# A fixed order for a stick-breaking attention layer: where the memory's split, the key norms and the projection chunks stand

## The chip, the core and the metric

The kernel runs on one NeuronCore of one Trainium2 chip. The metric is the device time of one execution in microseconds. Five engines work side by side, each through its own rows in order: TensorE (PE) multiplies, VectorE (DVE) and ScalarE (ACT) do elementwise work, GpSimd (POOL) helps with some of it, and SyncE (SP) issues the transfers of weights. An engine waits for another through semaphores.

## The reference

One step of a two-layer encoder over 256 prompt frames and 32 sample frames (288 columns in all), model width 1024, and 256 memory tokens. Layer 0 has two kinds of attention side by side, layer 1 the stick-breaking attention C. Behind the mixer, each layer has a cross-attention into the memory and an MLP. What matters here is C and the memory's keys for layer 1's cross-attention:

```python
def stick_breaking_attend(q, k, v, q_pos, k_pos):
    z = jnp.einsum('bqhd,bkhd->bhqk', q, k, preferred_element_type=jnp.float32) * (HEAD_DIM ** -0.5)
    before = k_pos[None, :] < q_pos[:, None]
    log_keep = jnp.where(before, jax.nn.log_sigmoid(-z), 0.0)
    tail = lax.cumsum(log_keep, axis=3, reverse=True) - log_keep
    w = jnp.where(before, jnp.exp(jax.nn.log_sigmoid(z) + tail), 0.0)
    return jnp.einsum('bhqk,bkhd->bqhd', w.astype(v.dtype), v)

def mem_kv(mem, g_mem, w_kv, k_gain):
    b, n, _ = mem.shape
    k, v = jnp.split(rmsnorm(mem, g_mem) @ w_kv, 2, axis=-1)
    k = rmsnorm(k.reshape(b, n, N_HEADS_X, HEAD_DIM_X), k_gain)
    return k, v.reshape(b, n, N_HEADS_X, HEAD_DIM_X)
...
        hp = hp + dp
        mk, mv = mem_kv(mem_prompt, norm_mem[layer], x_w_kv[layer], x_qk_gain[layer, 1])
        hp = hp + cross_attend(rmsnorm(hp, norm_cross[layer]), mk, mv, x_w_q[layer], x_qk_gain[layer, 0], x_w_o[layer])
        hp = hp + mlp(rmsnorm(hp, norm_mlp[layer]), mlp_w_up[layer], mlp_w_down[layer])
```

The memory's projection does not depend on the activations, so its work can stand nearly anywhere ahead of the cross-attention.

## The kernel before

**Layout and products.** Activations lie with features on the 128 partitions and the 288 frames along the row; the width of 1024 is eight blocks `k`. Weights come in chunks of 256 output columns. Each fp32 product is made of three (`mm3`, L158 to L160): every operand is split into a high part and a remainder, and high x high, high x low and low x high are added in a bank. A chunk is thus 2 x 8 x 3 = 48 products.

**Weights** (`load_chunk`, L117). A chunk arrives as two halves of 512 KB (`raw`, four buffers, L125, issued on SP). ACT copies a half to its high part `wh` (L143; for some pieces DVE does it, L141), DVE (or POOL) subtracts to get `wl` (L144). `wh` and `wl` have three buffers each. A transfer is issued when its `raw` buffer has been split; a split needs the buffer of the chunk half three before, which is free when PE's last product from it is done. ACT, DVE, POOL and SP get their order from a scheduler, which starts ready work by rank; `with ahead(n)` raises the rank of what is issued within it by n.

**C.** The class `Mix` (L575) issues the projections of C by a list, `ORD_C`: `q0` to `q3`, `k0` to `k3`, `v0` to `v3` for the four groups of four heads, `m0` to `m3` for the memory's keys of layer 1 (four heads), and `M` for the split of the memory itself (`mem_split`, L310 the two transfers `mraw` of 512 KB into `raw` buffers, L313 eight `mh` rows on ACT, L314 eight `ml` rows on DVE). Within C the order of PE is the order of the code. `attend_c` (L662) asks `Mix` for products at three places (`FILL_C`: 96 behind the scores, 30 behind the weights, 12 ahead of the sample's part), so that PE has products to do while ACT and DVE work on the scores. `later(n, fn)` puts `fn` behind the next n products.

The rows that the prediction speaks of:

- The norm of C's input (`Norm.rms`, L210 squares, L212 sums, L215 a product `ps_rs` with ones, L182 logarithm and L183 exponential give `rs`). Until `rs` is there, q0's two banks can't be read out (`qz`, L626), and of three banks for projections two are held.
- A memory key's norm: `tmk` (L656) reads the two banks of a chunk m; `xnorm_parts` (L354) makes squares on ACT (L358), their sum `sqx` on DVE (L359), a high part `sh` (L341) and a low part `sl` (L343); `mem_k_norm`, issued by `later(36, ...)`, adds both over the partitions with two products `ps_xn` (L348, L349) and scales the key (`mk`, L368).
- In `attend_c`: `sp` (L719), `spl` (L724), the scan `zsb` (L727) and `ws` (L728) on DVE; the output's parts `oh` (L517) and `ol` (L518), which free the score banks `zz` for the sample's product (L513).
- v: `vT` (L642) reads v's two banks, `turn_v` transposes it (L449) and copies it (`vt`, L452), 18 and 36 products later.

In `ORD_C`, M stands behind v1, with its eight blocks spread by twelve products each; m0 stands ahead of v2, m1 ahead of v3, and so on.

Of the kernel before, what the change touches and what calls it, by code (L numbers as in the profile page):

```python
# [15 lines left out]
NP_ = 256  # L16
# [13 lines left out]
HPG = 0  # L30
VT2 = 1
ORD_AB = 'qA0 pA0 F qA1 pA1 aA0 qB0 aA1 qB1 pB0 M pB1 aB0 N K2 aB1 K0 K3 K1'.split()
ORD_C = 'q0 k0 v0 q1 k1 v1 M q2 k2 m0 v2 q3 k3 m1 v3 m2 m3'.split()
FILL_C = 96, 30, 12
ORD_X = 's1 s2 s3 s0 v0 v1 S v2 v3'.split()
NWARM = 9
# [15 lines left out]
def body(ctx: ExitStack, tc: tile.TileContext, i: dict, o: dict):  # L52
# [94 lines left out]
    def ahead(n):  # L147
        return tc.high_priority(n) if n else ExitStack()
# [28 lines left out]
    def split_into(dh, dl, src):  # L177
        act(dh, src, AF.Copy)
        dve.tensor_tensor(dl, src, dh.bitcast(F32), ALU.subtract)
# [120 lines left out]
    def mem_split(layer, put=None):  # L300

        mh = spp.tile([P, KT, T], F32R, tag="sp", name="mh")
        ml = spp.tile([P, KT, T], F32R, tag="sp", name="ml")
        ssum = scr.tile([P, T], F32, tag="ssum", name="mssum", bufs=2) if layer == 0 else None
        raws = []

        def step(k):
            if k % 4 == 0:
                raws.append(wraw.tile([P, 4, NP_], F32, tag="raw", name="mraw"))
                nc.sync.dma_start(out=raws[-1], in_=i["memT"][:, k:k + 4, :])  # L310
            m = raws[-1][:, k % 4, :]
            g = gT[:, 3, layer, k:k + 1]
            act(mh[:, k, 0:NP_], m, AF.Copy, scale=g)  # L313
            dve.scalar_tensor_tensor(ml[:, k, 0:NP_], m, g, mh[:, k, 0:NP_].bitcast(F32), ALU.mult, ALU.subtract)  # L314
            if layer == 0:
                if k == 0:
                    act(ssum[:, 0:NP_], m, AF.Square)
                else:
                    sq = scr.tile([P, T], F32, tag="f", bufs=FB, name="sqm")
                    act(sq[:, 0:NP_], m, AF.Square)  # L320
                    dve.tensor_tensor(ssum[:, 0:NP_], ssum[:, 0:NP_], sq[:, 0:NP_], ALU.add)

        for k in range(KT):
            if put is None:
                step(k)
            else:
                put(k, lambda k=k: step(k))
        return mh, ml, ssum
# [9 lines left out]
    def two_parts(sq, n):  # L338

        sh = scr.tile([P, T], F32R, tag="f", bufs=FB, name="sh")  # L340
        dve.tensor_copy(sh[:, 0:n], sq[:, 0:n])  # L341
        sl = scr.tile([P, T], F32R, tag="f", bufs=FB, name="sl")
        (nc.gpsimd if HNP else dve).tensor_tensor(sl[:, 0:n], sq[:, 0:n], sh[:, 0:n].bitcast(F32), ALU.subtract)  # L343
        return sh, sl
# [9 lines left out]
    def xnorm_parts(t, n):  # L354
        sq = []
        for d in range(2):
            sq.append(scr.tile([P, T], F32, tag="f", bufs=FB, name="sqx"))
            act(sq[d][:, 0:n], t[:, d, 0:n], AF.Square)  # L358
        dve.tensor_tensor(sq[0][:, 0:n], sq[0][:, 0:n], sq[1][:, 0:n], ALU.add)  # L359
        return two_parts(sq[0], n)  # L360

    def xnorm_from(parts, t, n, gains, out):
        ps = bank(R.m, "ps_xn")
        add_parts(ps, onesr, parts, n)
        r = scr.tile([P, T], F32, tag="f", bufs=FB, name="rx")
        rstd_of(ps[:, 0:n], n, 1.0 / 256, r[:, 0:n])
        for d in range(2):
            dve.scalar_tensor_tensor(out[:, d, 0:n], t[:, d, 0:n], gains[:, d:d + 1], r[:, 0:n], ALU.mult, ALU.mult)  # L368
# [10 lines left out]
    def mem_k_norm(layer, hd, t, parts):  # L379
        k_ = memp.tile([P, 2, NP_], F32, tag="mk", name="mk", bufs=1)  # L380
        xnorm_from(parts, t, NP_, xqkg[:, layer, 1, :], k_)
        nc.gpsimd.dma_start(out=o["memkT"][:, layer, 2 * hd:2 * hd + 2, :], in_=k_)
        kh = memp.tile([P, 2, NP_], F32R, tag="mkh", name="mkh")
        kl = memp.tile([P, 2, NP_], F32R, tag="mkl", name="mkl")
        split_into(kh, kl, k_)
        return kh, kl
# [59 lines left out]
    def turn_v(vT, vt, p):  # L446
        pt = bank(ps_t, "ps_vt")
        for j in range(2):
            nc.tensor.transpose(pt[:, j * P:(j + 1) * P], vT[:, p, j * P:(j + 1) * P], ident)  # L449
        nc.tensor.transpose(pt[0:NS, 2 * P:3 * P], vT[:, p, NP_:T], ident)  # L450
        act(vt[:, 0:2, p * P:(p + 1) * P], pt[:, 0:2 * P].rearrange("p (j c) -> p j c", j=2), AF.Copy)
        act(vt[0:NS, 2, p * P:(p + 1) * P], pt[0:NS, 2 * P:3 * P], AF.Copy)  # L452
# [118 lines left out]
    class Mix:  # L571
# [44 lines left out]
        def run(self, steps):  # L616
            xh, xl, rs = self.x
            for step in steps:
                op, g = step[0], int(step[1:] or 0)
                if op == "M":  # L620
                    mem = mem_split(1, lambda k, fn: self.later(12 * k, fn))[0:2]
                elif op == "q":
                    qz = R.ph.tile([P, 2, T], F32, tag="qz", name="qz", bufs=QZB[1])
                    yield from self.products(i["sb_w"][g], xh, xl)
                    for p in range(2):
                        dve.scalar_tensor_tensor(qz[:, p, :], self.ps[p][:, 0:T], 0.125, rs, ALU.mult, ALU.mult)  # L626
                    self.done["q", g] = qz
                elif op == "k":
                    kT = R.ph.tile([P, 2, T], F32, tag="kT", name="kT", bufs=KTB[1])
                    yield from self.products(i["sb_w"][4 + g], xh, xl)  # L630
                    for p in range(2):
                        dve.tensor_tensor(kT[:, p, :], self.ps[p][:, 0:T], rs, ALU.mult)
                    nc.gpsimd.dma_start(out=o["ckT"][:, 2 * g:2 * g + 2, :], in_=kT)
                    self.done["k", g] = kT
                elif op == "v":
                    vT = scr.tile([P, 2, T], F32, tag="t2", name="vT")
                    vt = R.ph.tile([P, 3, CW], F32, tag="vt", name="vt", bufs=VTB)

                    nc.gpsimd.memset(vt[:, 2, :], 0.0)
                    yield from self.products(i["sb_w"][8 + g], xh, xl)  # L640
                    for p in range(2):
                        dve.tensor_tensor(vT[:, p, :], self.ps[p][:, 0:T], rs, ALU.mult)  # L642
                    nc.gpsimd.dma_start(out=o["cvT"][:, 2 * g:2 * g + 2, :], in_=vT)

                    def turn(p, vT=vT, vt=vt, g=g):
                        turn_v(vT, vt, p)
                        if p:
                            self.done["v", g] = vt

                    self.later(18, lambda turn=turn: turn(0))  # L650
                    self.later(36, lambda turn=turn: turn(1))
                else:
                    yield from self.products(i["w_kv"][1, g], *mem, NP_)
                    t = scr.tile([P, 2, T], F32, tag="t2", name="tmk")
                    for d in range(2):
                        dve.tensor_tensor(t[:, d, 0:NP_], self.ps[d][:, 0:NP_], memrs, ALU.mult)  # L656
                    parts = xnorm_parts(t, NP_)
                    self.later(36, lambda t=t, g=g, parts=parts: self.done.update({("m", g): mem_k_norm(1, g, t, parts)}))
            self.mem = mem

    def attend_c(g, qz, kT, vt, ck, cv, oh, ol, fill):
# [311 lines left out]
    for step in ORD_AB:  # L973
        op, at = step[0], step[1:]
        kind, g = ("AB".index(at[0]), int(at[1])) if len(at) == 2 else (0, 0)
# [32 lines left out]
    dve.tensor_scalar(big, ident, 2.0 ** 100, None, ALU.mult)  # L1008
    mix = Mix(ORD_C)
    mix.x = xh, xl, rs  # L1010
# [124 lines left out]
```

## Time and profile before

| | |
|---|---|
| median of 3 runs | 971.75 us (970.33 to 974.96) |
| profiled execution | 971.41 us |
| its span | 969.7 us |
| mean granted TensorE clock | 0.994 |
| weight halves of C's projections, 512 KB each | 24 transfers, median 3.8 us to landing |
| memory's halves, both layers | 4 transfers, median 3.9 us to landing |

The times are of the profiled execution unless the runs are named; the span leaves out 1.7 us around it. In rows of the timeline the columns are start, duration (both us), engine, line, operation, output and inputs with their sizes, and in brackets the idle time ahead of it and what ended it. C's first product (q0) starts at 493.39 us.

### The profile page before, as it was taken

How to read it: one execution, taken by the hardware profiler on the slowest of the kernel's cores; microseconds unless marked ns; L12 is line 12 of the kernel's file. 1: busy time of each engine (PE TensorE's matmuls, PEld its weight loads, DVE VectorE, ACT ScalarE, POOL GpSimd, SP SyncE). 2: the span in 40 equal slices, each digit the busy share in tenths (PEclk: the TensorE clock that was granted, in tenths of full speed). 3: DMA queues.
4: the chain of work that ended last, by engine and by line, in shares of the span. 5: the costliest groups of instructions: out<-in, count | busy, mean ns of one | idle time of the engine just before them, and what ended most of it. 6: DMA issues, size and time to landing. Idle time of an engine off the chain costs nothing.

```text
span 969.7 us, 19222 instructions
## 1 busy us (share of the span) xinstructions
PE 951.9 (98%) x7284; PEld 920.5 (95%) x7284; DVE 686.4 (71%) x1506; ACT 526.5 (54%) x1220; POOL 170.2 (18%) x200
## 2 busy tenths in 40 slices
PE   8999999999999999999999999899999999999998
PEld 7998899899999999999999899899999999999998
DVE  8779978679687767767766756677987766564643
ACT  5667667556456645454446754654544655454531
POOL 4002200022112211212100000003443111121110
PEclk9999999999999999999999999999999999999999
DMA  8654464654555555555445544465443455555452
GB/s 263 221 155 143 133 206 155 213 163 136 175 167 163 171 164 163 168 164 169 154 160 175 181 132 151 130 226 174 141 155 130 152 175 168 163 167 168 161 173 72
DMA packets 50700, 160.01 MB, mean 165 GB/s; under 512 B 6296, under 2 KB 12968, under 8 KB 50352
## 3 DMA queue, kind: packets, MB, share of 16 engines
q1 hardware_dynamic: 46864, 148.69, 47.8%
q0 software_dynamic: 2592, 8.92, 2.4%
q10 hardware_dynamic: 1152, 1.18, 0.4%
q8 instruction: 57, 0.93, 0.4%
q14 instruction: 35, 0.29, 0.1%
HBM read 148.65 MB, written 10.12 MB: 164 GB/s over the span
## 4 chain that ended last, share of the span: by engine, by line
PE 88%; DVE 5%; ACT 4%; DMA 2%; issue 1%; SPq 0%; DVEq 0%; ACTq 0%
PE g L158 26%; PE g L160 26%; PE g L159 26%; DVE wl L144 2%; DMA raw<-in_w_kv_dram 1%; PE po L503 1%; PE zz L736 1%; ACT wh L143 1%; PE zz L503 1%; ACT mh L313 1%; DMA h<-in_xT_dram 0%; ACT pr L491 0%; PE zz L691 0%; PE sx L158 0%; PE sx L160 0%
## 5 line engine op out<-in xcount | busy, mean ns | idle before, releaser
L143 ACT ACTIVATE wh<-raw 128x512 fp32r<-128x512 f32 (+3 forms) x541 | 269.4, 547 | 243.1 <-PE g L159 129.4
L144 DVE TENSOR_TENSOR wl<-raw,wh 128x512 fp32r<-128x512 f32 (+3 forms) x519 | 320.9, 655 | 103.4 <-ACT wh L143 96.9
L158 PE MATMUL g<-xh,wh 128*128 128x288 f32 (+1 forms) x1032 | 305.0, 300 | 3.6 <-DVE qz L626 1.6
L159 PE MATMUL g<-xl,wh 128*128 128x288 f32 (+1 forms) x1032 | 303.7, 297 | 1.5 <-DVE xl L196 1.5
L160 PE MATMUL g<-xh,wl 128*128 128x288 f32 (+1 forms) x1032 | 303.1, 297 | 0.8 <-DVE wl L144 0.8
L158 PEld LDWEIGHTS g<-xh,wh 128*128 128x128 f32 (+1 forms) x1032 | 192.7, 188 | 7.5 <-DVE qz L626 2.2
L144 POOL TENSOR_TENSOR wl<-raw,wh 128x256 fp32r<-128x256 f32 (+2 forms) x105 | 122.4, 1166 | 432.7 <-ACT wh L143 348.4
L159 PEld LDWEIGHTS g<-xl,wh 128*128 128x128 f32 (+1 forms) x1032 | 193.5, 188 | 3.0 <-DVE xl L196 2.5
L160 PEld LDWEIGHTS g<-xh,wl 128*128 128x128 f32 (+1 forms) x1032 | 193.2, 188 | 2.5 <-DVE wl L144 1.5
L159 PE MATMUL g<-hl,wh 128*128 128x288 f32 x512 | 150.3, 295 | 0.0
L158 PE MATMUL g<-hh,wh 128*128 128x288 f32 x512 | 149.0, 295 | 0.0
L160 PE MATMUL g<-hh,wl 128*128 128x288 f32 x512 | 148.7, 294 | 0.0
L159 PEld LDWEIGHTS g<-hl,wh 128*128 128x128 f32 x512 | 96.1, 188 | 0.0
L160 PEld LDWEIGHTS g<-hh,wl 128*128 128x128 f32 x512 | 95.8, 188 | 0.0
L158 PEld LDWEIGHTS g<-hh,wh 128*128 128x128 f32 x512 | 95.3, 187 | 0.0
L159 PE MATMUL g<-ol,wh 128*128 128x288 f32 x256 | 76.2, 299 | 0.0
L160 PE MATMUL g<-oh,wl 128*128 128x288 f32 x256 | 75.4, 298 | 0.0
L158 PE MATMUL g<-oh,wh 128*128 128x288 f32 x256 | 74.9, 298 | 0.3 <-ACT oh L522 0.3
L141 DVE CAST wh<-raw 128x256 fp32r<-128x256 f32 (+2 forms) x83 | 33.5, 404 | 46.2 <-PE g L159 26.8
L888 DVE TENSOR_TENSOR h<-h,g 128x288 f32<-128x288 f32 x64 | 28.8, 450 | 29.6 <-PE g L160 29.5
L159 PEld LDWEIGHTS g<-ol,wh 128*128 128x128 f32 x256 | 48.8, 191 | 0.8 <-issue 0.8
L160 PEld LDWEIGHTS g<-oh,wl 128*128 128x128 f32 x256 | 48.6, 191 | 0.0
(285 smaller groups left out, 1471.2 us busy)
## 6 DMA issues: line engine op xcount, KB each, us to landing
raw<-in_w_up_dram SPq DMA_DIRECT2D x64, 512.0 KB, 3.8
raw<-in_w_down_dram SPq DMA_DIRECT2D x64, 512.0 KB, 3.8
raw<-in_w_kv_dram SPq DMA_DIRECT2D x32, 512.0 KB, 3.9
raw<-in_sb_w_dram SPq DMA_DIRECT2D x24, 512.0 KB, 3.8
raw<-in_ab_w_dram SPq DMA_DIRECT2D x22, 512.0 KB, 4.8
raw<-in_w_q_dram SPq DMA_DIRECT2D x16, 512.0 KB, 4.0
raw<-in_w_o_dram SPq DMA_DIRECT2D x16, 512.0 KB, 3.9
raw<-in_ab_wo_dram SPq DMA_DIRECT2D x8, 512.0 KB, 3.9
```

The costliest lines, as they stand in the source:

```text
L141: dve.tensor_copy(wh[:, r, :], src)
L143: act(wh[:, r, :], src, AF.Copy)
L144: e.tensor_tensor(wl[:, r, :], src, wh[:, r, :].bitcast(F32), ALU.subtract)
L158: mm(out, lh, rh, start=first, stop=False)
L159: mm(out, lh, rl, start=False, stop=False)
L160: return mm(out, ll, rh, start=False, stop=last)
L313: act(mh[:, k, 0:NP_], m, AF.Copy, scale=g)
L503: mm(po[64 * par:64 * par + 64, kk * P:NP_], vt[:, kk, cols], pts[par][kk], start=kk == 0, stop=kk == 1)
L736: mm(zz[:, e, 0:384], mtrir, x[:, e, :], stop=False, **k_)
L888: dve.tensor_tensor(h[:, kt, :], h[:, kt, :], ps[:, 0:T], ALU.add)
```

## The change

Four edits, all in C:

```diff
-ORD_C = 'q0 k0 v0 q1 k1 v1 M q2 k2 m0 v2 q3 k3 m1 v3 m2 m3'.split()
+ORD_C = 'M q0 k0 v0 q1 k1 v1 m0 q2 k2 v2 m1 q3 k3 v3 m2 m3'.split()
...
                 if op == "M":
-                    mem = mem_split(1, lambda k, fn: self.later(12 * k, fn))[0:2]
+                    mem = mem_split(1)[0:2]
...
-                    parts = xnorm_parts(t, NP_)
-                    self.later(36, lambda t=t, g=g, parts=parts: self.done.update({("m", g): mem_k_norm(1, g, t, parts)}))
+                    with ahead(400):
+                        parts = xnorm_parts(t, NP_)
+                    self.later(48, lambda t=t, g=g, parts=parts: self.done.update({("m", g): mem_k_norm(1, g, t, parts)}))
```

The memory is split all at once, ahead of q0. Each memory chunk of the first two stands ahead of a group's q, and v directly behind its k. A key norm's squares, their sum and its two parts get a rank higher by 400, and its two products come 12 products later. Behind L656 the lines of the changed kernel are numbered one higher. No instruction is added or removed.

SP, at the end of layer 0's MLP and the start of C. `raw` are weight halves, `mraw` memory's; before:

```order
L125 DMA raw_6534<-in_w_down_dram 128x1024
L125 DMA raw_6546<-in_w_down_dram 128x1024
L125 DMA raw_6671<-in_sb_w_dram 128x1024
L125 DMA raw_6679<-in_sb_w_dram 128x1024
L125 DMA raw_6740<-in_sb_w_dram 128x1024
L125 DMA raw_6748<-in_sb_w_dram 128x1024
```

And of the change:

```order
L125 DMA raw_6534<-in_w_down_dram 128x1024
L125 DMA raw_6546<-in_w_down_dram 128x1024
L310 DMA mraw_6672<-in_memT_dram 128x1024
L310 DMA mraw_6682<-in_memT_dram 128x1024
L125 DMA raw_6693<-in_sb_w_dram 128x1024
L125 DMA raw_6701<-in_sb_w_dram 128x1024
```

Memory's two transfers now stand where q0's two halves (6671 and 6679 before, 6693 and 6701 now) stood; the queue behind is two places later.

ACT, where the norm of C's input is finished (`rs_6653`). The `wh` rows are splits of k0's second half (6750 before, 6772 now) and v0's first half (6816, 6838). Before:

```order
L210 ACTIVATE sq_6648<-h_100 128x288
L143 ACTIVATE wh_6750<-raw_6748 128x512
L182 ACTIVATE rs_6653<-ps_rs_6651,epsb_105 128x288
L143 ACTIVATE wh_6816<-raw_6814 128x512 x2
L183 ACTIVATE rs_6653<-rs_6653 128x288
L680 ACTIVATE qs_6860<-qz_6670,m01_255 128x2x32 x2
```

And of the change:

```order
L210 ACTIVATE sq_6648<-h_100 128x288
L143 ACTIVATE wh_6772<-raw_6770 128x512
L143 ACTIVATE wh_6838<-raw_6836 128x512 x2
L182 ACTIVATE rs_6653<-ps_rs_6651,epsb_105 128x288
L183 ACTIVATE rs_6653<-rs_6653 128x288
L681 ACTIVATE qs_6882<-qz_6692,m01_255 128x2x32 x2
```

The pair of splits of v0's first half moved from between the logarithm and the exponential to ahead of both. On PE, the product `ps_rs` stands seven rows later than before, with two products of q0 and k0 between it and the first one that needs a bank that `qz` frees, where there were nine.

DVE, at the key norm of m1 (before, the one of L343 at which PE waits). Before:

```order
L359 TENSOR_TENSOR sqx_8055<-sqx_8055,sqx_8057 128x256
L141 CAST wh_8160<-raw_8158 128x512
L719 SCALAR_TENSOR_TENSOR sps_7997<-zsb_7996 128x288
L341 CAST sh_8060<-sqx_8055 128x256
L724 TENSOR_TENSOR spl_8022<-sp_8004,sph_8021 128x768
L144 TENSOR_TENSOR wl_8161<-raw_8158,wh_8160 128x512 x2
L727 SCALAR_TENSOR_TENSOR zsb_7996<-sps_7997 128x288
L343 TENSOR_TENSOR sl_8062<-sqx_8055,sh_8060 128x256
```

And of the change:

```order
L656 TENSOR_TENSOR tmk_7802<-g_7740,memrs_264 128x256
L656 TENSOR_TENSOR tmk_7802<-g_7741,memrs_264 128x256
L729 TENSOR_TENSOR ws_7667<-zsb_7665 128x288
L144 TENSOR_TENSOR wl_7927<-raw_7924,wh_7926 128x512 x2
L359 TENSOR_TENSOR sqx_7805<-sqx_7805,sqx_7807 128x256
L341 CAST sh_7810<-sqx_7805 128x256
L343 TENSOR_TENSOR sl_7812<-sqx_7805,sh_7810 128x256
L141 CAST wh_7934<-raw_7932 128x512
```

The sum of squares and its two parts now are neighbours; what stood between them stands ahead or behind.

In group 0, the two `ol` rows of L518, which had six `ml` rows (L314) between them, are neighbours as well, since the memory's split has gone to the front.

## The prediction

> **What bounds the kernel now.** I read the top of the page first: span, busy shares, and the chain that ended last.
>
> ```profile
> span 969.7 us, 19222 instructions
> PE 951.9 (98%) x7284; PEld 920.5 (95%) x7284; DVE 686.4 (71%) x1506; ACT 526.5 (54%) x1220; POOL 170.2 (18%) x200
> PE 88%; DVE 5%; ACT 4%; DMA 2%; issue 1%; SPq 0%; DVEq 0%; ACTq 0%
> ```
>
> TensorE is busy for 98% of the span and carries 88% of the chain. The change alters no product, so all it can win or lose is PE's waits and its clock. It leaves the first layer's mixer and cross-attention alone; PE's order differs only between the last chunk of layer 0's MLP and the start of layer 1's cross-attention. So the second view is PE's waits in 440 to 680 us. Columns: engine, waiting tile and line, what released it, then us in total, times, longest.
>
> ```profile
> PE ps_xn L349 <- DVE sl L343: 2.6, 1, 2.6
> PE g L158 <- DVE qz L626: 1.6, 1, 1.6
> PE zz L513 <- DVE ol L518: 1.1, 1, 1.1
> PE g L158 <- DVE vT L642: 0.8, 1, 0.8
> PE ps_vt L449 <- ACT vt L452: 0.2, 1, 0.2
> ```
>
> These five waits are the whole stake: 6.3 us by this column. The third view is the timeline around the longest.
>
> ```profile
> 617.45 0.35 PE L348 MATMUL ps_xn<-sh,onesr 128*128 128x256 f32 x1
> 620.41 0.53 PE L349 MATMUL ps_xn<-sl,onesr 128*128 128x256 f32 x1 [2.61 <-DVE sl L343]
> ```
>
> The column counts idle time after a product's pipelined end. From start to start the loss is larger: 620.41 - 617.45 = 2.96, and two products normally start about 0.13 apart, so 2.8 us is lost where the column says 2.6. I add 0.2 to each wait: 2.8, 1.8, 1.3, 1.0, 0.4. The fourth view is busy time by stretch, which has the granted clock (the column of 1.00 or 0.50) behind the engines' busy times (PE, PEld, DVE, ACT, POOL). The edges are those at which the clock changes in this trace, 3.41 us apart.
>
> ```profile
> 6.09:9.51 3.42, 2.12 (x13) 1.67 (x12) 3.35 (x10) 1.96 (x5) 2.03 (x4) 1.00 0.92 247
> 9.51:12.92 3.41, 2.36 (x12) 1.43 (x12) 3.41 (x5) 2.65 (x7) 2.66 (x3) 1.00 0.50 150
> 12.92:16.34 3.42, 3.42 (x15) 3.40 (x15) 3.35 (x17) 2.59 (x8) 0.00 (x0) 0.50 1.00 334
> 501.03:504.45 3.42, 1.80 (x14) 1.63 (x13) 2.02 (x4) 1.48 (x5) 0.00 (x0) 1.00 0.36 117
> 504.45:507.86 3.41, 3.41 (x28) 3.41 (x27) 1.72 (x3) 0.64 (x1) 0.00 (x0) 1.00 0.24 84
> 617.09:620.50 3.41, 0.80 (x5) 0.39 (x3) 3.41 (x8) 0.00 (x0) 0.00 (x0) 1.00 0.53 157
> 620.50:623.91 3.41, 3.41 (x15) 3.41 (x16) 1.52 (x5) 1.52 (x4) 0.00 (x0) 0.50 0.46 150
> ```
>
> [...] The stretch of the 2.6 us wait held 5 products, and the next ran 15 where a full one runs 28: half of 3.41, **1.7 us** more, belongs to that wait. With 13 (at 6.09) and 14 products (at 501.03, the wait for `qz`) the clock stayed; with 12 (at 9.51) it fell, though PE counts as busy for longer there: the products count, not the busy time. [...]
>
> **The change part by part.** *Key norms.* In the row of 620.41 PE waits for `sl`, the low half of a key norm's summed squares. On DVE, between `sh` and `sl`, stood work of other parts:
>
> ```profile
> 618.09 1.28 DVE L144 TENSOR_TENSOR wl<-raw,wh 128x512 fp32r<-128x512 f32 x2
> 619.29 0.75 DVE L727 TENSOR_TENSOR_SCAN zsb<-sps 128x288 f32<-128x288 f32 x1
> 619.96 0.39 DVE L343 TENSOR_TENSOR sl<-sqx,sh 128x256 fp32r<-128x256 f32 x1
> ```
>
> The changed order has `sqx`, `sh`, `sl` in three neighbouring rows right behind `tmk` and one weight split, and PE asks for them twelve products later. They end about 3 us or more before PE's turn at all four norms, by my walk through the order with these durations. Gone: 2.8 us and, with it, the 1.7 us of clock. If a split pair (1.28) slipped in again, the slack would still cover it.
>
> *Memory out of group 0.* Before, memory's low halves stood between the two `ol` rows of group 0.
>
> ```profile
> 539.69 0.48 DVE L314 SCALAR_TENSOR_TENSOR ml<-mraw,gT,mh 128x256 fp32r<-128x256 f32 x1
> 540.09 0.42 DVE L518 TENSOR_TENSOR ol<-zz,oh 128x256 fp32r<-128x256 f32 x1
> 540.56 0.66 PE L513 MATMUL zz<-wts,cv 128*64 128x32 f32 x16 [1.11 <-DVE ol L518]
> ```
>
> Now the two `ol` rows are neighbours: the 1.3 us go. What is late next there is nothing in the order with a price.
>
> *Chunks by group.* In group 2 PE waited for `vT` (1.0) and soon after for `vt` (0.4):
>
> ```profile
> 584.87 0.40 PE L158 MATMUL g<-xh,wh 128*128 128x288 f32 x1 [0.85 <-DVE vT L642]
> ```
>
> v's products now stand around the scores, with `vT` right behind DVE's `sp` rows, so both waits go: 1.4. New is that in groups 2 and 3 `tmk` stands behind the scan (0.75, above) while PE needs `tmk`'s bank: I take 0.2 twice, and 0.2 for group 1, whose `ol` stands behind a key's `mk`: 0.6 in all, between 0 and 2 (the scan's 0.75 in full, twice, and half a microsecond).
>
> *Memory ahead of q0.* Its eight `ml` rows (0.48 each, as above) and eight `mh` copies are not new work, they move. They now stand among the splits of the last down chunk, and memory's two transfers take the queue places of q0's two halves. SP's rows:
>
> ```profile
> 476.99 3.31 SPq L125 DMA_DIRECT2D raw<-in_sb_w_dram  x2
> 483.50 9.04 SPq L125 DMA_DIRECT2D raw<-in_sb_w_dram  x4
> ```
>
> Before, q0 and k0 were asked for at 476.99 to 486.3 or so, each transfer as a buffer came free. After, q0's first half follows the split of the last down chunk, by my walk at 485.7, its second at 489.8, with k0's two halves right behind, since memory's buffers are free by then.
>
> ```profile
> raw<-in_sb_w_dram SPq DMA_DIRECT2D x24, 512.0 KB, 3.8
> raw<-in_sb_wo_dram SPq DMA_DIRECT2D x1, 512.0 KB, 4.2
> 493.39 0.30 PE L158 MATMUL g<-xh,wh 128*128 128x288 f32 x1
> ```
>
> The first half lands at 489.5, ahead of q0's first product at 493.39. The second lands at 493.6 to 494.0: 3.8 is the median of such transfers, and 4.2 that of one with four more issued right behind it. DVE's cast of it stands ahead of the `h` sum that frees q0's second bank, needed about 495.3; by my walk 0.5 us to spare, **after which lateness costs one for one**.
>
> *The wait for `qz`* stays, and this is the part I am least sure of.
>
> ```profile
> 499.37 0.65 PE L215 MATMUL ps_rs<-ssum,ones 128*128 128x288 f32 x2
> 500.05 0.50 ACT L182 ACTIVATE rs<-ps_rs,epsb 128x288 f32<-128x288 f32 x1 [2.59 <-PE ps_rs L215]
> 500.45 1.14 ACT L143 ACTIVATE wh<-raw 128x512 fp32r<-128x512 f32 x2
> 500.91 0.29 PE L160 MATMUL g<-xh,wl 128*128 128x288 f32 x1
> 501.10 1.29 DVE L144 TENSOR_TENSOR wl<-raw,wh 128x512 fp32r<-128x512 f32 x2 [2.50 <-ACT wh L143]
> 501.49 0.43 ACT L183 ACTIVATE rs<-rs 128x288 f32<-128x288 f32 x1
> 502.31 0.81 DVE L626 SCALAR_TENSOR_TENSOR qz<-g,rs 128x288 f32<-128x288 f32 x2
> 502.82 0.40 PE L158 MATMUL g<-xh,wh 128*128 128x288 f32 x1 [1.62 <-DVE qz L626]
> ```
>
> From `ps_rs` to PE's return it was 502.82 - 499.37 = 3.45. Now the pair of `wh` splits stands ahead of the logarithm on ACT. It waits for the product just ahead of `ps_rs`: start 0.2 behind `ps_rs`, 1.14 long; then 0.45 and 0.43 for `rs`; DVE's `wl` pair ends meanwhile, at 2.2; `qz` 2.25, PE 0.5 later: 2.75, so 0.7 less. But `ps_rs` stands 7 products later (0.13 each, 0.9), with 2 products behind it as cover, before 9. Net +0.2. DVE has little to spare: k0's second half is split only just ahead, some 2 us later than before, and any more lateness goes through. I take **+0.4**, between -0.2 (the splits come early) and +1.5 (the `wl` pair, 1.29, wholly in the way). The gap from product to product grows from 502.82 - 500.91 = 1.9 to 2.3.
>
> *The sum.* Gone 2.8 + 1.3 + 1.4 = 5.5; new 0.6 + 0.4 = 1.0; clock -1.7. The profiled execution took 971.41 (span 969.7), 0.3 under the median of the runs shown, 971.75. 971.4 - 5.5 + 1.0 - 1.7 = **965.2**.
>
> **The rivals.** *The clock falls at `qz` instead.* With a gap of 2.3, a stretch that holds all of it has (3.41 - 2.3) / 0.13 + 1 = 9 or 10 products, under the 12 that sufficed at 9.51. The stretches' edges lie where they lie: the gap falls whole, or up to 0.3 short of whole at one side, into one stretch for (1.1 + 0.6) / 3.41 = half of the positions; some discount is due, as +0.2 would be nearly as before. Then 1.7 is paid there: **966.9**.
>
> [...]
>
> *Slower: q0's second half lands late.* If the transfers issued within 2 us of it share the engines instead of following in order, three or four end together. Estimate: a lone transfer lands in 3.8, and each further one adds 1.6 (512 KB at the 334 GB/s of the stretch at 12.92), so q0's half lands at 489.8 + 3.8 + 2 x 1.6 = 496.8, with part of a fourth 497.5. PE waits 3.4 instead of having 0.5 to spare, the clock falls there (1.7) and at `qz` (1.7): 965.2 + 6.8 = **972.0**, slower than 971.4. It decides from a landing at about 497 on. Against it: the 4.2 us row, with four transfers behind it.
>
> *It doesn't do what it says:* one key norm still waits, because another row on DVE or ACT ends late ahead of its `sl`. The 2.8 stay, with or without the 1.7: 968.0 to **969.7**. For it: four norms and only my walk for their slack. Against it: three neighbouring rows.
>
> **How the numbers follow.** Forecast 965.2, within 1.3, chance 0.43. Clock lost at `qz`, 966.9 within 1.3: 0.33. A key norm still waits: 0.08. Late transfer: 0.05. Better than forecast (no new small waits, `qz` earlier): 0.05. Something unseen that gives back more: 0.06. The range holds the first two with their bounds and most of the third: 963.2 to 970.3, about 0.85. Half a per cent, about what a measurement of this kernel can tell from no change, is 4.9 us: faster means under 966.9, slower over 976.6. Faster: 0.38 of the forecast's 0.43, half of the second case's 0.33, 0.05 of the better: 0.60. Slower: 0.03, the late transfer at its worst and half of the unseen. The rest, 0.37, is within.
>
> **What would show it.** In the profile after, PE's waits should have no row for `ps_xn` or `vT`, and for `zz` at most 0.3; the row for `qz` about 2.0. The granted clock is 1.00 around the key norms. If the stretch behind `qz` shows 0.50, the first rival is right; if PE waits in q0 for an `h` sum or a `wh`, the second; a row for `sl` over 1 us, the third. The prediction is wrong if waits of over 1 us appear in places not named here, or if the clock doesn't follow the count of products.

## The result, and the profile after

| | before | changed |
|---|---|---|
| median of 20 runs each | 971.13 us (968.53 to 976.74) | 966.91 us (962.87 to 970.20) |
| ratio, with its 95% interval | | 0.995 (0.9936 to 0.9964) |
| profiled execution | 971.41 us | 964.98 us |
| its span, its mean granted clock | 969.7 us, 0.994 | 963.3 us, 0.998 |

The change gains 4.2 us by the medians, and the interval gives 3.5 to 6.2. The two profiled executions lie 6.4 us apart: the profiled one of the changed kernel is a quick one of its kind. Part of what sets it apart is the clock: a second trace of the same kernel, below, has a half clock in C, and its C is 1.5 us longer. One execution of the first experiment took 2344.14 us, which no trace explains, and is left out of that experiment's median and ratio.

The page of the changed kernel, its top:

```profile
span 963.3 us, 19227 instructions
PE 947.7 (98%) x7284; PEld 916.5 (95%) x7284; DVE 685.9 (71%) x1506; ACT 526.3 (55%) x1220; POOL 172.3 (18%) x200
PE 88%; DVE 6%; DMA 2%; ACT 2%; issue 1%; SPq 0%; DVEq 0%; ACTq 0%
```

The same products, but PE is busy for 4.2 us less: half-clock stretches count as busy (in the one at 620.50 of before PE is busy for all of its 3.41 us, with 15 products). Apart from the end of the run, the trace of before has half clock in the stretches that start at 12.92, 176.76 and 620.50 us, that of the changed kernel in the one at 7.52; of these only the one at 620.50 lies in C. PE's waits in 440 to 680 us, changed kernel:

```profile
PE g L158 <- DVE qz L626: 1.9, 1, 1.9
PE g L158 <- DVE tmk L656: 0.3, 1, 0.3
```

Five rows have become two: `ps_xn`, `zz`, `vT` and `vt` are gone, `qz` grew by 0.3, a small one for `tmk` is new. The wait for `qz` in the timeline of the changed kernel (PE, then ACT and DVE):

```profile
499.86 0.65 PE L215 MATMUL ps_rs<-ssum,ones 128*128 128x288 f32 x2
500.13 0.64 PE L160 MATMUL g<-xh,wl 128*128 128x288 f32 x2
502.67 0.40 PE L158 MATMUL g<-xh,wh 128*128 128x288 f32 x1 [1.90 <-DVE qz L626]
...
500.11 1.15 ACT L143 ACTIVATE wh<-raw 128x512 fp32r<-128x512 f32 x2 [2.83 <-PE g L159]
501.17 0.48 ACT L182 ACTIVATE rs<-ps_rs,epsb 128x288 f32<-128x288 f32 x1
501.68 0.44 ACT L183 ACTIVATE rs<-rs 128x288 f32<-128x288 f32 x1
...
500.77 1.29 DVE L144 TENSOR_TENSOR wl<-raw,wh 128x512 fp32r<-128x512 f32 x2 [1.79 <-ACT wh L143]
502.15 0.82 DVE L626 SCALAR_TENSOR_TENSOR qz<-g,rs 128x288 f32<-128x288 f32 x2
```

From `ps_rs` to PE's return it is 502.67 - 499.86 = 2.81 us, where before it was 3.45; but only two products follow `ps_rs` as cover. The key norm of m1, first on DVE, then on PE:

```profile
590.84 0.42 DVE L359 TENSOR_TENSOR sqx<-sqx 128x256 f32<-128x256 f32 x1
591.29 0.29 DVE L341 CAST sh<-sqx 128x256 fp32r<-128x256 f32 x1
591.62 0.43 DVE L343 TENSOR_TENSOR sl<-sqx,sh 128x256 fp32r<-128x256 f32 x1
...
597.75 0.28 PE L348 MATMUL ps_xn<-sh,onesr 128*128 128x256 f32 x1
597.87 0.28 PE L349 MATMUL ps_xn<-sl,onesr 128*128 128x256 f32 x1
```

`sl` is done at 592.05 and PE takes it at 597.87, 5.8 us later. Where in the program did the two profiled executions part? The norm's product `ps_rs` at the end of C is a mark in both; first before, then changed:

```profile
672.88 0.41 PE L215 MATMUL ps_rs<-ssum,ones 128*128 128x288 f32 x1
```

```profile
492.96 0.30 PE L158 MATMUL g<-xh,wh 128*128 128x288 f32 x1
666.36 0.41 PE L215 MATMUL ps_rs<-ssum,ones 128*128 128x288 f32 x1
```

From q0's first product to that mark: 672.88 - 493.39 = 179.49 before, 666.36 - 492.96 = 173.40 after. C is 6.1 us shorter in these two executions, and all of the rest differs by 0.3.

### The profile page after: what moved, and what is told of

Its sections match the earlier page's. It is cut to its first block, busy times and chain, and to the rows that moved or that the text cites. A ratio compares the mean times of both kernels' runs of the same rounds, so it can differ in the third digit from the quotient of the medians.

```text
span 963.3 us, 19227 instructions
## 1 busy us (share of the span) xinstructions
PE 947.7 (98%) x7284; PEld 916.5 (95%) x7284; DVE 685.9 (71%) x1506; ACT 526.3 (55%) x1220; POOL 172.3 (18%) x200
## 4 chain that ended last, share of the span: by engine, by line
PE 88%; DVE 6%; DMA 2%; ACT 2%; issue 1%; SPq 0%; DVEq 0%; ACTq 0%
PE g L158 26%; PE g L160 26%; PE g L159 26%; DVE wl L144 2%; DMA raw<-in_w_kv_dram 1%; PE po L503 1%; PE zz L737 1%; PE zz L692 1%; PE zz L503 1%; ACT wh L143 1%; DMA bsmp<-cd 0%; ACT pr L491 0%; DMA raw<-in_ab_w_dram 0%; DVE spl L725 0%; PE sx L158 0%
## 5 line engine op out<-in xcount | busy, mean ns | idle before, releaser
L158 PEld LDWEIGHTS g<-oh,wh 128*128 128x128 f32 x256 | 47.5, 188 | 0.6 <-ACT oh L522 0.4
```

Source lines behind the costliest of these rows:

```text
L158: mm(out, lh, rh, start=first, stop=False)
```

## The experiments

Two questions were open: which of the four edits brings which part, and why the medians show 4.2 us where the two traces show 6.4. Two theories on the key norms: A, the rank and the twelve products took the wait away; B, the new list did. Two on the clock: the gain of 1.7 us behind the key norm comes in full; or the half clock comes at `qz` instead.

**The key norms' two edits alone.** The kernel before with

```diff
-                    parts = xnorm_parts(t, NP_)
-                    self.later(36, ...
+                    with ahead(400):
+                        parts = xnorm_parts(t, NP_)
+                    self.later(48, ...
```

> The kernel before with only the two edits on the key norms (the rank of the squares, and 48 instead of 36 products); the list and the spread of the memory's split are the old ones. Theory A, that these two edits remove the wait at the key norm by themselves: the row ps_xn <- sl (2.6 us) is gone, no half clock behind it, so 2.8 us faster and in executions that had the half clock 4.5 us (ratio 0.995 to 0.997). Theory B, that the new list does it and the rank alone moves little: on DVE the cast, spl, a split pair and the scan still stand between sqx and sl, only the twelve products (12 x 0.13 = 1.6 us) are new cover, so about 1.0 us of the 2.6 us stay in that row and it is 1.6 us faster (ratio about 0.998). Both: the rows for qz (1.6), ol (1.1) and vT (0.8) stay.

Measured: 967.00 us (median of eleven), ratio 0.9971 (0.9956 to 0.9986), which fits both theories; the rows decide. The four longest of PE's waits in this kernel, and DVE's rows at the key norm of m1:

```profile
PE g L158 <- DVE qz L626: 1.6, 1, 1.6
PE ps_xn L349 <- DVE sl L343: 1.3, 1, 1.3
PE zz L513 <- DVE ol L518: 1.1, 1, 1.1
PE g L158 <- DVE vT L642: 0.5, 1, 0.5
```

```profile
617.27 0.28 DVE L341 CAST sh<-sqx 128x256 fp32r<-128x256 f32 x1
617.47 0.95 DVE L725 TENSOR_TENSOR spl<-sp,sph 128x768 fp32r<-128x768 f32 x1
618.34 1.29 DVE L144 TENSOR_TENSOR wl<-raw,wh 128x512 fp32r<-128x512 f32 x2
619.55 0.75 DVE L728 TENSOR_TENSOR_SCAN zsb<-sps 128x288 f32<-128x288 f32 x1
620.22 0.40 DVE L343 TENSOR_TENSOR sl<-sqx,sh 128x256 fp32r<-128x256 f32 x1
```

Theory B holds: with the rank higher by 400, the same rows stand between `sh` and `sl` as before. Only the twelve products act, and half of the wait stays. From q0 to the mark this trace takes 669.87 - 494.04 = 175.83 us, 3.7 less than before. The shorter wait for `sl` gives 1.4 of it from start to start and a shorter one for `vT`, which the expectation did not have, 0.4; no half clock follows the shorter wait (its stretch, from 617.59, holds 16 products, and the next one is at 1.00 with 31), which makes up the rest. The runs agree: their mean clock is 0.9975, that of the kernel before beside them 0.9955.

**The new list without the key norms' edits.** The changed kernel with

```diff
-                    with ahead(400):
-                        parts = xnorm_parts(t, NP_)
-                    self.later(48, ...
+                    parts = xnorm_parts(t, NP_)
+                    self.later(36, ...
```

> The changed kernel without the two edits on the key norms: the new list, the memory split at once in front, but the old rank and 36 products. Theory A: the wait for sl comes back, 1 to 2.6 us, with a half clock behind it in some executions: 1 to 4 us slower than the changed kernel. Theory B: no wait for sl over 0.3 us; the time of the changed kernel within 0.5 us, so a ratio to the kernel before of 0.994 to 0.996.

Measured: 965.86 us, ratio 0.9952 (0.9935 to 0.9969), the ratio of the whole change. PE's waits of this kernel:

```profile
PE g L158 <- DVE qz L626: 1.9, 1, 1.9
PE g L158 <- DVE tmk L656: 0.3, 1, 0.3
```

The same two rows as in the changed kernel. At the key norm of m1, `sl` is done at 592.34 and PE takes it at 596.57, 4.2 us later. The edits on the key norms are not needed: the list moved this memory chunk to a place where DVE has nothing in the way.

**The memory's split moved back.** The changed kernel with

```diff
-ORD_C = 'M q0 k0 v0 q1 k1 v1 m0 q2 k2 v2 m1 q3 k3 v3 m2 m3'.split()
+ORD_C = 'q0 k0 v0 M q1 k1 v1 m0 q2 k2 v2 m1 q3 k3 v3 m2 m3'.split()
...
-                    mem = mem_split(1)[0:2]
+                    mem = mem_split(1, lambda k, fn: self.later(12 * k, fn))[0:2]
```

> The changed kernel with the memory's split moved back from in front of q0 to behind v0 and spread by 12 products again (list q0 k0 v0 M q1 k1 v1 m0 ...). If the move to the front is what lengthens the wait for qz: the row is 1.6 again (1.9 in the changed kernel), 0.3 us less; memory's rows stand ahead of group 0's scores and cost nothing, so no row for ol: 0.3 us faster than the changed kernel, ratio to the kernel before 0.993 to 0.996. Rival, that the front was needed: a row for ol of about 1.1 us or a new one in q1, k1 or v1 of 0.5 us or more, 1 us slower than the changed kernel.

Measured: 966.91 us, ratio 0.9964 (0.9951 to 0.9978). Its waits:

```profile
PE g L158 <- DVE qz L626: 2.0, 2, 1.6
PE g L158 <- DVE kT L632: 0.9, 1, 0.9
PE g L158 <- DVE vT L642: 0.7, 1, 0.7
PE g L158 <- DVE tmk L656: 0.3, 1, 0.3
```

The first half of the expectation came true (the longest wait for `qz` is 1.6 again), and so did the rival: eight `ml` rows among the first projections make PE wait for `kT`, `vT` and a second `qz`, 2.0 us in all. DVE's rows ahead of the wait for `kT`:

```profile
507.84 0.48 DVE L314 SCALAR_TENSOR_TENSOR ml<-mraw,gT,mh 128x256 fp32r<-128x256 f32 x1
508.23 0.81 DVE L632 TENSOR_TENSOR kT<-g,rs 128x288 f32<-128x288 f32 x2
```

The median is about 1 us over that of the same list with the memory in front (965.86), with intervals that overlap. From q0 to the mark it takes 668.05 - 492.17 = 175.88 us in its trace, without any half clock (its mean clock is 1.000; the stretch of the wait for `qz`, from 498.51, holds 13 products), 2.5 more than the changed kernel in its first trace. In front of q0 DVE has the room.

**The memory in front alone.** The kernel before with

```diff
-ORD_C = 'q0 k0 v0 q1 k1 v1 M q2 k2 m0 v2 q3 k3 m1 v3 m2 m3'.split()
+ORD_C = 'M q0 k0 v0 q1 k1 v1 q2 k2 m0 v2 q3 k3 m1 v3 m2 m3'.split()
...
-                    mem = mem_split(1, lambda k, fn: self.later(12 * k, fn))[0:2]
+                    mem = mem_split(1)[0:2]
```

> The kernel before with only the memory's split moved in front of q0, at once; the rest of the list and the key norms are old. By the sum of waits: ol's 1.3 us gone, qz 0.3 us longer, ps_xn (2.6) and vT (0.8) stay: 1.0 us faster than before (ratio 0.999), within what a measurement tells. Rival, that the place of the memory is the main part of the gain: 3 us or more faster. [...]

Measured: 969.67 us, ratio 0.9993 (0.9981 to 1.0005), as the sum of waits had it and not clear of no change: `ol` is gone, `ps_xn` (2.6), `qz` (1.9) and `vT` (0.8) are there. The place of the memory by itself is not what gains. Two stretches of this trace, each with the one behind it:

```profile
499.52:502.93 3.41, 1.51 (x11) 1.28 (x10) 2.12 (x4) 2.33 (x6) 0.00 (x0) 1.00 0.52 175
502.93:506.34 3.41, 3.41 (x16) 3.41 (x15) 0.79 (x2) 0.63 (x1) 0.00 (x0) 0.50 0.33 119
615.58:618.99 3.41, 1.58 (x11) 1.17 (x9) 3.41 (x8) 0.59 (x2) 0.00 (x0) 1.00 0.50 154
618.99:622.40 3.41, 2.63 (x11) 2.63 (x12) 2.09 (x6) 1.30 (x4) 0.00 (x0) 0.50 0.51 159
```

Here the clock was halved twice, behind `qz` and behind the key norm; each time 11 products lay in the stretch, whole or in part. C takes 673.40 - 492.13 = 181.27 us in this trace, longer than before in spite of the shorter waits. The 179.49 of before, less 1.0 of waits, with 1.3 for the second half clock (half of PE's 2.63 us), make 179.8; the 1.5 left would be one more half-clock stretch, an estimate that no row here shows.

**The changed kernel again,** on the chip of the three runs that follow it, without an edit.

> The changed kernel once more, beside the three that follow, on their chip. Waits of the first profile: qz 1.9, tmk 0.3, nothing else in C. Theory A (the time is the sum of PE's waits, and the half clock behind the wait for qz comes in some executions only): ratio to the kernel before 0.994 to 0.996; mean granted clock about 0.996, where the kernel before has 0.9955. Theory B (the clock gain of 1.7 us comes in full in every execution): ratio 0.9935, clock 0.0018 above that of the kernel before.

Measured: 965.51 us, ratio 0.9958 (0.9946 to 0.9971); mean granted clock over its executions 0.9963, over those of the kernel before beside it 0.9960. A clock lower by 0.0018 is one half-clock stretch (half of 3.41 us in 965), so the gain of the clock is a fifth of a stretch. Each of the two means has a standard error of 0.0003, so one whole stretch is unlikely, and none at all is not excluded. The same wait of 1.9 us stands in both traces of the changed kernel, and the clock behind it differs. The first trace:

```profile
499.04:502.45 3.41, 1.73 (x12) 1.39 (x10) 1.59 (x3) 1.98 (x4) 0.00 (x0) 1.00 0.60 198
502.45:505.87 3.42, 3.20 (x24) 3.20 (x25) 1.07 (x4) 1.22 (x3) 0.00 (x0) 1.00 0.47 168
```

This one:

```profile
498.80:502.21 3.41, 1.51 (x10) 1.17 (x9) 2.12 (x4) 2.19 (x5) 0.00 (x0) 1.00 0.57 184
502.21:505.62 3.41, 3.41 (x16) 3.41 (x16) 0.00 (x0) 0.38 (x2) 0.00 (x0) 0.50 0.43 151
```

In the first, the end of the gap reached into the next stretch, and 12 products were left in its own; in this one the gap lay whole in one stretch with 10. Of four traces with a wait of 1.9 us (two of the changed kernel, the new list alone, the memory in front alone) three have the half clock behind it.

What the half clock costs can be read from the length of C, which in this trace is 666.85 - 491.95 = 174.90 us:

```profile
491.95 0.30 PE L158 MATMUL g<-xh,wh 128*128 128x288 f32 x1
666.85 0.41 PE L215 MATMUL ps_rs<-ssum,ones 128*128 128x288 f32 x1
```

The first trace has 173.40 with the same waits, so the half clock at `qz` costs 1.5 us. Against the 179.49 of before, C is 4.6 us shorter here, near the 4.2 of the medians. The whole execution is only 0.5 us longer than the first (965.47 and 964.98), because its q0 starts 1.0 us earlier; in the ten traces q0 starts anywhere from 491.76 to 494.11 us, and that scatter ahead of C is in every median.

**The split of v0 behind the exponential.** The changed kernel with v0's weight splits on ACT queued behind the exponential of C's norm (`R.rs` is that instruction):

```diff
...
+            with tc.issue_after(pin) if pin is not None else ExitStack():
-            ws = load_chunk(ap)
+                ws = load_chunk(ap)
...
-                    yield from self.products(i["sb_w"][8 + g], xh, xl)
+                    yield from self.products(i["sb_w"][8 + g], xh, xl, pin=R.rs if g == 0 else None)
```

> The changed kernel with the splits of v0's two halves on ACT queued behind the exponential of C's norm, so that neither they nor their subtractions on DVE stand between ps_rs and qz. If those rows are what the wait for qz is made of: from ps_rs 0.65, then logarithm and exponential 0.9, qz and back 0.55, in all 2.1 us instead of 2.8, so the row for qz 1.2 to 1.3 (1.9 in the changed kernel). A gap that leaves 16 products or more in its stretch never halves the clock: 0.7 us of wait and up to 0.8 us of clock on average, so 0.7 to 1.5 us faster than the changed kernel. Rival, that v0's splits are then late: a row for wh or wl in v0 of 0.5 us or more, and nothing gained.

Measured: 963.86 us, ratio 0.9937 (0.9925 to 0.9949), 1.6 us under the changed kernel beside it; mean clock 0.9978. The wait and its stretch:

```profile
PE g L158 <- DVE qz L627: 1.3, 1, 1.3
```

```profile
499.93:503.34 3.41, 2.11 (x16) 1.88 (x15) 2.02 (x4) 2.46 (x6) 0.00 (x0) 1.00 0.36 130
503.34:506.76 3.42, 3.42 (x28) 3.42 (x27) 1.83 (x4) 0.64 (x1) 0.00 (x0) 1.00 0.48 158
```

The row, the count and the clock are as expected: 0.6 us of wait gone, 16 products in a stretch that holds the whole gap, and a clock that stays at 1.00. That 16 or more never halve it is not shown: in the trace of before a stretch with 34 products, 24 of them of 128x32 only, was followed by 0.50 (last section). C takes 665.23 - 492.44 = 172.79 us, 0.6 less than the changed kernel without half clock and 2.1 less than with it. The gain of 1.6 us is just above the expected 0.7 to 1.5. It lies between the two, as if the changed kernel paid the 1.5 us in about two of three executions; that is an estimate, from medians of five and six. No row for v0's splits appeared.

**The wait made longer.** The changed kernel with

```diff
             rstd_of(ps[:, 0:T], T, 1.0 / 1024, rs)
+            if self.at == (0, 1):
+                for _ in range(3):
+                    act(rs, rs, AF.Copy)
```

> The changed kernel with three copies of rs onto itself on ACT behind the exponential (about 0.4 us each, the values stay), so that the wait for qz is 1.2 us longer: 3.1 in its row. If the clock follows the products in a stretch of 3.41 us (12 or fewer halve the next), a gap of 3.4 us halves the clock wherever the stretches lie, so in all executions a half clock follows, in the profile too: 1.2 us of wait and 0.6 to 1.0 us of clock on average, so 1.8 to 2.2 us slower than the changed kernel, and its mean clock 0.0005 to 0.001 lower. Rival, that the clock has nothing to do with this wait: 1.2 us slower, the same mean clock.

Measured: 966.53 us, ratio 0.9967 (0.9953 to 0.9980), mean clock 0.9958. Its wait, and its stretch:

```profile
PE g L158 <- DVE qz L629: 3.3, 1, 3.3
```

```profile
501.99:505.40 3.41, 0.15 (x1) 0.15 (x2) 1.90 (x4) 2.59 (x6) 0.00 (x0) 1.00 0.63 195
505.40:508.81 3.41, 3.41 (x15) 3.41 (x16) 0.16 (x1) 0.59 (x2) 0.00 (x0) 0.50 0.18 68
```

The wait came out 1.4 us longer, and the half clock is there, but the median moved by 1.0 us only, where 1.8 to 2.2 was expected: if the changed kernel pays for the half clock in most executions already, little is left to lose. The mean clock fell by 0.0005, within its noise. C takes 670.46 - 494.11 = 176.35 us, 1.45 more than in the second trace of the changed kernel: with half clock in both, the wait alone. This miss fits the reading that the half clock at `qz` is the commoner case in the changed kernel. With 12 and 6 executions it does not show it.

**The scan behind `tmk`.** The kernel of the run with v0's splits behind the exponential, and

```diff
-                        dve.tensor_tensor(t[:, d, 0:NP_], self.ps[d][:, 0:NP_], memrs, ALU.mult)
+                        R.tmk = dve.tensor_tensor(t[:, d, 0:NP_], self.ps[d][:, 0:NP_], memrs, ALU.mult).ins
...
-        dve.tensor_tensor_scan(su[:, ::-1], sps[:, ::-1], sps[:, ::-1], 0.0, ALU.add, ALU.max)
-        dve.tensor_tensor(ws[:, 0:T], z, su, ALU.subtract)
-        act(ws[:, 0:T], ws[:, 0:T], AF.Exp)
+        R.tmk = None
         fill(FILL_C[0])
+        with tc.issue_after(R.tmk) if R.tmk is not None else ExitStack():
+            dve.tensor_tensor_scan(su[:, ::-1], sps[:, ::-1], sps[:, ::-1], 0.0, ALU.add, ALU.max)
+            dve.tensor_tensor(ws[:, 0:T], z, su, ALU.subtract)
+        act(ws[:, 0:T], ws[:, 0:T], AF.Exp)
```

> As the run with v0's splits behind the exponential, and DVE's scan and its difference are queued behind the two tmk rows of their group. If the scan ahead of tmk is what PE waits for in the row for tmk (0.3, with two gaps of 0.4 and 0.3 from product to product): both gaps gone, 0.5 to 0.7 us faster than that run. Rival, that the scan's own user (the transposes of ws) is then late: a row for ps_ws of 0.3 us or more and nothing gained.

Measured: 962.43 us, ratio 0.9929 (0.9917 to 0.9942), the lowest median of the kernels here. Its waits in C:

```profile
PE g L158 <- DVE qz L627: 1.3, 1, 1.3
PE g L158 <- DVE tmk L657: 0.3, 1, 0.3
```

Half of the expectation: the row of 0.3 is still there. It is group 1's, where `spl` and not the scan stands ahead of `tmk`; the two smaller gaps of groups 2 and 3 (0.24 and 0.28 over the usual distance of two products, too small for that list) are gone. Against the run without this edit the median is 1.4 us lower, more than the 0.5 us of these gaps, and the two intervals overlap. From q0 to the end of the span it is 468.8 us in its trace, 0.9 less than the 469.7 without this edit. The rest stays open: with the edit the order of PE's rows in group 3 changed too.

## Why the prediction was right, point by point

The measured 966.91 us lies in the range, 1.7 us over the forecast of 965.2. The waits were right; one step was mis-sized, the clock.

- **Key norms.** The wait went, as said. The slack, "about 3 us or more" at all four norms, is 5.0, 5.8, 5.2 and 3.4 us. What the step left open is which edit does it: that `sqx`, `sh`, `sl` are neighbours comes from the list alone. The rank does nothing to these rows under the old list, and the twelve products there leave 1.3 us.
- **Memory out of group 0.** The wait for `ol` went. That "nothing" is late next there held: no new row appeared in group 0. With the memory in front alone, the sum gave 1.0 us, and the medians differ by 1.1.
- **Chunks by group.** Both waits (`vT`, `vt`) went. The new small waits were put at 0.6; over the usual distance of two products they are 0.42, 0.24 and 0.28, 0.9 in all, and all three are `tmk`'s; none came behind a key's `mk` in group 1.
- **The front.** q0's second half was said to be asked for at 489.8 and to land at 494.0. The changed kernel's list of transfers in 485.0 to 485.3 has that one, with its size and its time to landing; on SP it is the first of the merged timeline row below it:

```profile
raw<-in_sb_w_dram SPq DMA_DIRECT2D x1, 512.0 KB, 4.9
```

```profile
485.16 14.23 SPq L125 DMA_DIRECT2D raw<-in_sb_w_dram  x7
```

  Issued at 485.16 and landed 4.9 later, at 490.1: the walk was too late by 4 us, and the slower rival never came near.

- **The wait for `qz`.** From `ps_rs` to PE 2.75 was worked out, 2.81 measured; the row was put at about 2.0 and is 1.9. The gap from product to product, 502.67 - 500.48 = 2.2 (500.48 is the start of the second of the two products behind `ps_rs`), was put at 2.3.
- **The sum of waits.** Forecast 5.5 gone and 1.0 new. From start to start, less the usual 0.13, the trace of before has 2.8, 1.8, 1.3, 1.0, 0.3 and one more of 0.3 for a second `qz`, that of the changed kernel 2.1, 0.4, 0.3 and 0.2: 7.5 against 3.0, so 4.5 us less, the forecast's own number.
- **The clock.** The step "clock -1.7" is the one that was too large. It took the half clock behind the key norm as gone and put a second one, at `qz`, into a rival with 0.33. Behind `qz` it came in one of the two traces of the changed kernel and in both others with the same wait. The mean clock rose by 0.0001 to 0.0006 only (0.9961 over 20 executions, against 0.9955 over 30 and 0.9960 over 17 of the kernel before, in other sets of runs). That is 0.1 to 0.6 us instead of 1.7; with it the sum is 4.6 to 5.1 us, inside the interval of the result. By the length of C the two cases stand apart. The forecast's, 179.49 - 4.5 - 1.7 = 173.3, is the first trace (173.40), and the rival's, 1.7 more, is the second (174.90). Both were real. By the gain of the pin the second is the commoner, and it had been given the smaller chance, by a count of positions that allowed a discount for a change of a few tenths in the gap. Just there the two traces part: 12 products in the stretch with 1.00 behind it, 10 with 0.50 behind it. That 12 suffice was an estimate from the one row at 9.51. How often the kernel before pays at the key norm was not measured by itself; its one trace does, and the clock of the first experiment suggests that most executions do (0.9975, against 0.9955).
- **Luck.** The first rival's price was 966.9, and the median is 966.91. So close a match is luck: the scatter ahead of C alone is larger, and the median mixes both cases. That the sum of waits comes out to 0.1 us owes something to two misses that cancel: 5.7 gone (with a second `qz` that the forecast did not have) and 1.2 new, where 5.5 and 1.0 were forecast.

## What to carry to other kernels

When PE is the bound, list its waits and price each from start to start; the sum of these was right to 0.1 us here. Then look, for each wait, at the granted clock of the stretch behind it: the same wait of 1.9 us had 1.00 behind it in one trace of the changed kernel and 0.50 in the other, with 1.5 us between the two in C, and one profile shows only one of the cases. To compare two traces, take the distance between two marks around the change: here it showed to 0.1 us what the scatter ahead of it hid in the whole time. And before a rank or a delay is added, look whether the order of the work alone already clears the place: two of the four edits here (the rank and the twelve products) were idle, and a pin of one engine's row behind another was worth 1.6 us by the medians.

## What the runs showed of the hardware

Some stretches of 3.41 us that held a wait, with products of 128x288 (at the key norm a few of 128x256 among them), counted whole or in part: those with 1 (the wait made longer, from 501.99), 5 (before, 617.09), 10 (the changed kernel again, 498.80, and the new list alone, 498.59) and 11 (the memory in front alone, 499.52 and 615.58) were followed by one at 0.50. Those with 13 (before, 6.09; the key norms' two edits, 501.35; the memory moved back, 498.51), 14 (before, 501.03) and 16 (the key norms' two edits, 617.59; v0 behind the exponential, 499.93) were followed by one at 1.00. With 12 it was 0.50 once (before, 9.51) and 1.00 once (the changed kernel, 499.04). No run shows a fixed limit, such as the "12 or fewer" of an expectation. In three of four traces a wait of 1.9 us was followed by 0.50. The rows show this and not the time: the prediction's sum without any clock term, 971.4 - 5.5 + 1.0, is 966.9 as well.

The prediction's "the products count, not the busy time" is too wide. In the trace of before, 34 products, 24 of them of 128x32 only, were followed by half clock too, with PE busy for 2.19 us:

```profile
173.35:176.76 3.41, 2.19 (x34) 1.73 (x33) 1.34 (x3) 1.50 (x4) 0.39 (x1) 1.00 0.22 82
176.76:180.18 3.42, 3.42 (x17) 3.42 (x16) 1.64 (x4) 1.76 (x4) 0.00 (x0) 0.50 0.90 314
```

So the count holds for the rows above at most; what the clock follows in general is not shown here.

The stretch behind, where it was halved at `qz` or the key norm, ran 15 (before, from 620.50; the wait made longer, from 505.40) or 16 products (three more traces, behind `qz`) where a full one at 1.00 ran 28 (before, from 504.45), and 11 where the rest of the wait lay in it (memory in front alone, from 618.99).
